# A two-layer encoder trunk on one core: down projections of two pairs each, the last pair's plain products added into the same banks, and two of four weight sums written by a plain and an accumulating transfer

## The chip, the core and the metric

The kernel runs on one core of a Trainium2 chip. Its engines each work through a queue of their own in program order: TensorE (PE; PEld is its loading of weights) does matmuls into PSUM, VectorE (DVE) and ScalarE (ACT) work element by element, GpSimd (POOL) does little here, and SyncE (SP) issues transfers. The metric is the device time of one execution in microseconds; less is better.

## The reference

Two groups of tokens (512 and 256) of width 1024 go through two layers with shared weights. Each layer is a half feed-forward block, a mixer (gated spatial mixing beside windowed attention in the first layer, neighbourhood attention in the second) and another half feed-forward block; a final norm ends it. The change concerns the four feed-forward blocks:

```python
def rmsnorm(x, g):
    x32 = x.astype(jnp.float32)
    y = x32 * lax.rsqrt(jnp.mean(x32 * x32, axis=-1, keepdims=True) + EPS)
    return y.astype(x.dtype) * g
...
def swiglu(h, wg, wu, wd):
    return (jax.nn.silu(h @ wg) * (h @ wu)) @ wd
...
    x = x + 0.5 * swiglu(rmsnorm(x, f1_n), f1_g, f1_u, f1_d)
```

`wg` and `wu` are 1024 x 2816, `wd` is 2816 x 1024, all in float32.

## The kernel before

**Numbers.** A float32 operand is split into a rounded part (hi) and the remainder (lo), and each product is three matmuls: hi x hi, hi x lo, lo x hi (`mm3`, L184). A weight is split by `wsplit` (L105): ScalarE copies to `whi`, VectorE subtracts to `wlo`. There are five buffers of each, so splits run a few products ahead.

**Layout.** x lies transposed, features on the partitions in 8 tiles `x0` to `x7` of 768 tokens. The tokens are two halves of 384 (`HALVES`); all matmuls of the blocks have 384 columns.

**Pairs.** The 2816 hidden features are 11 pairs of 128-wide tiles. For a pair, the gate and the up projection are each a 2 x 2 block product (two halves of the 1024 inputs by two tiles, two halves of tokens), done in 7 products in place of 8, with sums on both sides: operand sums `t1`, `t2`, `t3`, `n4` beside the plain `b11`, `b21`, `b22` (made once per block by `feed` and `rest`), and weight sums s1 = a21 + a22, s2 = s1 - a11, s3 = a11 - a21, s4 = a12 - s2 (`sums`, L577), where a11 to a22 are 512 columns (a quarter) of the weights. A product of one projection is 12 matmuls (4 x `mm3`); `p1` to `p7` do both projections. s1 and s2 are made when `p6` (operand t2) asks for s2, s3 for `p7`, s4 for `p3`; s1 is used in `p5`. The seven results are joined in the banks X, Y, Z and in SBUF tiles, and `hidden` (L474) makes silu(gate) x up for each quarter of the pair's hidden values; it reads the bank of the last product (`sg<-ps_mm`, `v<-ps_mm`).

**Order.** TensorE's order is as written; the other engines' order comes from a scheduler. The first three pairs (`EARLY`) do their plain products `p1`, `p2` first, for all three, while the sums on the operand side are still being made; then their other five products follow pair by pair. Generators (`rest`, `second`, `norm_rt`) are advanced between products.

**Down.** Hidden values are summed and split per pair by `operands` (L400). `down` (L599) does 7 products per pair with the same four weight sums, accumulating over its pairs in one bank: pair 0 alone after pair 1, then pairs (1,2), (3,4), (5,6), (7,8), each two pairs later. Z is kept in `acc` over all of them and added to x by `last_operands` (L650). Pairs 9 and 10 go through `down_last` (L664) with plain products: for each of 8 output tiles and 2 halves 4 x `mm3` in an aux bank, then `x` is updated and `final` (L695) does what the next stage needs (the norm's squares, and the next operands: `feed` before a feed-forward block, `xh`/`xl` before a mixer). `half_done` then spawns the norm's tail, in which POOL takes a power (L254) and TensorE transposes its result (`ident,sm`).

**Loads.** Each 128 x 1024 weight tile comes as one 512 KB transfer on SP into one of four `raw` buffers (`raw`, L88). The sums lie in 8 buffers `s`.

Of the kernel before, what the change touches and what calls it, by code (L numbers as in the profile page):

```python
# [15 lines left out]
P = 128  # L16
# [32 lines left out]
class Trunk:  # L49
# [55 lines left out]
    def wsplit(self, src, eng=None, keep=False):  # L105
# [8 lines left out]
        hi, lo = (t.rearrange("p (a b) -> p a b", a=src.shape[1]) for t in (hi, lo))  # L114
        nc.scalar.copy(hi, src)  # L115
# [181 lines left out]
    def feed(self, m, h):  # L297
# [17 lines left out]
        if k in self.tmp and k + 4 in self.tmp:  # L315
            t2 = self.tmp["t2", k] = self.etile("tmp")
            self.combine(t2, self.tmp[k], -1, k, self.tmp[k + 4])
# [4 lines left out]
    def gain_split(self, n, k, src, m):  # L322

        hi, lo = self.b[n][k]
        self.nc.scalar.activation(hi, src, AF.Copy, scale=self.gain(m))
        self.nc.vector.scalar_tensor_tensor(
            out=lo, in0=src, scalar=self.gain(m), in1=hi.bitcast(F32), op0=ALU.mult, op1=ALU.subtract
        )

    def combine(self, out, x, sign, m, other):  # L330

        g, op = (self.gain(m), ALU.subtract) if sign > 0 else (self.gain(m, self.ngains), ALU.add)
# [11 lines left out]
    def rest(self, after):  # L344
# [5 lines left out]
        for n in ("t3", "t1", "b22", "n4"):  # L350
            for k in range(4):
                with self.tc.issue_after(self.copied[after - 1]) if after else nullcontext():
# [6 lines left out]
                    elif n == "n4":  # L359
                        t = self.tmp["t2", k]  # L360
                        self.combine(t, self.x[k + 4][:, a0:a1], 1, k + 4, t)
# [27 lines left out]
    def ffn(self, pre):  # L389
# [8 lines left out]
        d, dl = {}, {}  # L398

        def operands(q):  # L400
# [3 lines left out]
            sub = lambda o, x, y: nc.vector.tensor_tensor(out=o, in0=x, in1=y, op=ALU.subtract)  # L404
            d[q] = {}

            def put(n, src):
                d[q][n] = self.dtile(n), self.dtile(n)
# [4 lines left out]
            yield sub(h11, h12, h11)  # L413
            yield put("t1", h11)
            yield put("b21", h21)
            yield sub(h11, h22, h11)
            if q and q % 2 == 0:
                self.later = operands_2(h, sub, put)
                return
            for _ in operands_2(h, sub, put):  # L420
                yield

        def operands_2(h, sub, put):
# [5 lines left out]
            yield sub(h21, h21, h11)  # L429
            yield put("n4", h21)  # L430

        def pair(p):
# [5 lines left out]
            def load(tiles):  # L438
                for n in names:
                    for i in tiles:  # L440
                        r = self.first.pop(0) if self.first else self.raw(f"{pre}_w_{n}", 0, KD, (2 * p + i) * P, P)
                        a[n, i + 1, 1], a[n, i + 1, 2] = r[:, 0:4, :], r[:, 4:8, :]
# [5 lines left out]
            def sums(n, name):  # L448
                return self.sums(a[n, 1, 1], a[n, 1, 2], a[n, 2, 1], a[n, 2, 2], s, n, name)
# [24 lines left out]
            def hidden(i, half, g, u):  # L474
# [6 lines left out]
                nc.scalar.activation(t, t, AF.Silu)  # L481
                nc.vector.tensor_tensor(out=v, in0=u, in1=r, op=ALU.mult)
                nc.vector.scalar_tensor_tensor(out=t, in0=t, scalar=0.5, in1=v, op0=ALU.mult, op1=ALU.mult)  # L483
# [60 lines left out]
            load((0, 1))  # L544
            if p:
                steps = operands(p - 1) if p < NPAIR - 1 else self.last_operands(dl, 0, hs[p - 1], acc)
# [10 lines left out]
        for p in range(NPAIR):  # L557
            for _ in stages[p]:
                pass
            if p == 1:  # L560
                acc += [self.fw.tile([P, H], F32, tag=f"p1{j}", name=f"p1{j}") for j in range(4)]
            if p % 2 and p < NPAIR - 1:
# [1035 lines left out]
```

## Time and profile before

| | |
|---|---|
| median of 3 runs | 2640.08 us (2638.77 to 2641.93) |
| the profiled execution | 2645.25 us, of it the span of the program 2643.5 us |
| granted TensorE clock, mean | 0.993 |
| TensorE busy | 2586.7 us (98%), 15180 matmuls |
| VectorE busy | 2225.4 us (84%) |
| ScalarE busy | 1357.5 us (51%) |
| POOL busy | 97.6 us (4%) |
| transfers | 214.27 MB, mean 81 GB/s |

A row of a group names the line, engine, operation, out<-in and shape, then the count, busy time, mean ns of one, and the idle time of the engine just before them with what ended it. `L141` is the line of every matmul, so matmuls are told apart by tiles: `t20h,whi` is the rounded weight against the rounded operand t2 of input tile 0, the first matmul of that product. In a row of the timeline stand start, duration, engine, line and, in brackets, the idle time before it.

### The profile page before, as it was taken

To read this page: it belongs to the slowest core of one execution; us is meant where nothing else is said; L and a number is where in the kernel's file an instruction comes from. 1 tells how busy PE (TensorE), PEld (TensorE's weight loads), DVE (VectorE), ACT (ScalarE), POOL (GpSimd) and SP (SyncE) were. 2 spreads that over 40 slices of the span, in tenths; PEclk is the share of its full clock that TensorE was granted. 3 is DMA by queue.
4 is the path that set the end of the run, shared out by engine and by line. 5 is a ranking of instruction groups with operands and counts; after the bars stand their busy time and mean duration, and the time that the engine had idled before them with its cause. 6 is when DMAs were issued, how large, how long until landed. Compare 5 with 4: busy or idle time off the path is not lost.

```text
span 2643.5 us, 40905 instructions
## 1 busy us (share of the span) xinstructions
PE 2586.7 (98%) x15180; PEld 2515.4 (95%) x15180; DVE 2225.4 (84%) x4447; ACT 1357.5 (51%) x2808; POOL 97.6 (4%) x139
## 2 busy tenths in 40 slices
PE   8999999999999999999999999999999999999998
PEld 7899999987898999999999999998998989999998
DVE  8988889878869988889898888985667589888886
ACT  6545444546746544545654544464555455454443
POOL 0000000000000000000000000002212100000000
PEclk9999999999999999999999999999999999999999
DMA  5433222321132222223232222232112222222221
GB/s 156 125 81 93 80 73 71 126 89 51 47 101 91 80 65 79 67 78 96 64 96 64 76 69 75 69 129 80 60 62 72 80 80 80 80 65 80 64 81 63
DMA packets 83176, 214.27 MB, mean 81 GB/s; under 512 B 20128, under 2 KB 32928, under 8 KB 82976
## 3 DMA queue, kind: packets, MB, share of 16 engines
q1 hardware_dynamic: 82832, 211.62, 25.8%
q8 instruction: 119, 1.95, 0.3%
q14 instruction: 81, 0.66, 0.1%
q10 hardware_dynamic: 144, 0.03, 0.0%
HBM read 202.18 MB, written 15.07 MB: 82 GB/s over the span
## 4 chain that ended last, share of the span: by engine, by line
PE 68%; DVE 4%; ACT 2%; issue 1%; DMA 1%; POOL 0%; DVEq 0%; ACTq 0%; SPq 0%; POOLq 0%
PE ps_mm L141 42%; PE ps_aux L141 25%; PE ps_aux L152 1%; DMA raw<-in_w 1%; DVE wlo L116 1%; DVE s L579 1%; DVE ol L205 0%; ACT whi L115 0%; DVE tmp L333 0%; DVE x L631 0%; ACT ug L1157 0%; ACT L1157 0%; ACT p L884 0%; ACT L884 0%; DVE sg L483 0%
## 5 line engine op out<-in xcount | busy, mean ns | idle before, releaser
L115 ACT CAST whi<-s 128x512 fp32r<-128x512 f32 x496 | 301.7, 620 | 392.8 <-DVE s L579 142.8
L115 ACT CAST whi<-raw 128x512 fp32r<-128x512 f32 x512 | 312.5, 619 | 284.9 <-PE ps_mm L141 134.1
L116 DVE TENSOR_TENSOR wlo<-s,whi 128x512 fp32r<-128x512 f32 x496 | 336.0, 686 | 77.3 <-ACT whi L115 75.2
L116 DVE TENSOR_TENSOR wlo<-raw,whi 128x512 fp32r<-128x512 f32 x494 | 335.8, 686 | 38.6 <-ACT whi L115 35.9
L141 PE MATMUL ps_mm<-db,whi 128*128 128x384 f32 x864 | 221.3, 337 | 0.0
L141 PE MATMUL ps_aux<-dt,whi 128*128 128x384 f32 x864 | 221.3, 337 | 0.0
L141 PEld LDWEIGHTS ps_aux<-dt,whi 128*128 128x128 f32 x864 | 156.8, 188 | 0.0
L141 PEld LDWEIGHTS ps_mm<-db,whi 128*128 128x128 f32 x864 | 156.8, 188 | 0.0
L141 PE MATMUL ps_aux<-dt,wlo 128*128 128x384 f32 x432 | 145.7, 337 | 0.4 <-DVE wlo L116 0.4
L141 PE MATMUL ps_mm<-db,wlo 128*128 128x384 f32 x432 | 145.6, 337 | 0.0
L141 PE MATMUL ps_mm<-xh,whi 128*128 128x512 f32 (+1 forms) x416 | 145.3, 349 | 0.0
L141 PE MATMUL ps_mm<-xl,whi 128*128 128x512 f32 (+1 forms) x416 | 141.0, 339 | 0.0
L141 PE MATMUL ps_mm<-xh,wlo 128*128 128x512 f32 (+1 forms) x416 | 140.9, 339 | 0.0
L466 ACT COPY u<-ps_mm 128x384 f32<-128x384 f32 x176 | 83.5, 475 | 41.6 <-PE ps_mm L141 41.4
L471 DVE TENSOR_TENSOR u<-ps_aux,u 128x384 f32<-128x384 f32 x176 | 97.3, 553 | 6.9 <-PE ps_aux L141 4.5
L579 DVE TENSOR_TENSOR s<-raw 128x512 f32<-128x512 f32 x124 | 85.1, 686 | 17.3 <-DMA raw<-in_w 17.2
L579 DVE TENSOR_TENSOR s<-raw,raw 128x512 f32<-128x512 f32 x124 | 83.3, 686 | 19.4 <-DMA raw<-in_w 19.4
L141 PE MATMUL ps_aux<-dh,whi 128*128 128x384 f32 x384 | 98.9, 339 | 0.0
L631 DVE TENSOR_TENSOR x<-ps_aux,x 128x384 f32<-128x384 f32 x160 | 86.9, 554 | 12.3 <-PE ps_aux L141 12.2
L884 ACT ACTIVATE p<-p,st 128x256 f32<-128x256 f32 (+3 forms) x144 | 69.1, 481 | 47.8 <-DVE st L879 47.7
L631 DVE TENSOR_TENSOR x<-ps_mm,x 128x384 f32<-128x384 f32 x160 | 87.1, 552 | 6.0 <-PE ps_mm L141 6.0
L141 PEld LDWEIGHTS ps_mm<-xh,whi 128*128 128x128 f32 x416 | 78.9, 190 | 9.8 <-issue 1.0
(477 smaller groups left out, 8030.8 us busy)
## 6 DMA issues: line engine op xcount, KB each, us to landing
raw<-in_w SPq DMA_DIRECT2D x338, 512.0 KB, 3.7
xdm<-x SPq DMA_DIRECT2D x16, 384.0 KB, 2.4
raw<-in_w SPq DMA_DIRECT2D x16, 256.0 KB, 4.0
x<-in_x SPq DMA_DIRECT2D x16, 192.0 KB, 4.6
xold<-xdm SPq DMA_DIRECT2D x8, 384.0 KB, 3.0
x<-xdm SPq DMA_DIRECT2D x8, 384.0 KB, 3.5
out_y<-y SPq DMA_DIRECT2D x8, 384.0 KB, 2.6
tab<-skew SPq DMA_DIRECT2D x8, 256.0 KB, 4.2
```

Source lines behind the costliest of these rows:

```text
L115: nc.scalar.copy(hi, src)
L116: (eng or nc.gpsimd).tensor_tensor(out=lo, in0=src, in1=hi.bitcast(F32), op=ALU.subtract)
L141: self.nc.tensor.matmul(out, lhsT=lhsT, rhs=rhs, start=start, stop=stop, **kw)
L152: self.nc.tensor.transpose(out, src, self.ident)
L466: nc.scalar.copy(e[n, out], bank[key, n])
L471: nc.vector.tensor_tensor(out=t, in0=bank[key, n], in1=t, op=ALU.add)
L579: f = lambda o, x, y, op: self.nc.vector.tensor_tensor(out=o, in0=x, in1=y, op=op)
L631: nc.vector.tensor_tensor(out=o, in0=ps, in1=o, op=ALU.add)
L884: nc.scalar.activation(outs[i - n0], outs[i - n0], AF.Exp, scale=-1.0, bias=mn[:, i : i + 1], accum_out=sm[:, i : i + 1])
```

## The change

**Sums by transfer.** s1 and s3 are no longer made on VectorE: SP loads one quarter into a buffer `s`, and POOL issues a second transfer that adds the other quarter to it in memory. Signs are changed so that every sum is an addition: s2 = s1 + a11 and s4 = a12 + s2 stay on VectorE, s3 = a11 + a21, and the operand sums t1, t2, n4, the hidden values of a pair's second tile and the outputs of tiles 4 to 7 carry the sign. A quarter that is used in a sum and by itself is loaded for each use; `region` names a weight region without loading it, and `parts` loads quarters into a `raw` buffer.

**Down in twos.** `down` runs after pairs 2, 4, 6 and 8 for pairs (0,1), (2,3), (4,5), (6,7). `down_last` does pairs (8,9) in 7 products and adds the plain products of pair 10 into the same banks before these are read. Z is kept for the earlier pairs only, and is added to half 1 of x by `steps_last`. `out` calls `final`, as `one` did. Before a feed-forward block or the last norm (`lag`) the order is as written below; before a mixer it is other.

```diff
+    def region(self, name, k0, nk, c0, n):
+        size = P * nk * n
+        self.units.append((name, k0, nk, c0, n))
+        src = self.aps["w"][self.woff : self.woff + size].rearrange("(p f) -> p f", p=P)
+        self.woff += size
...
+        return src
+    def parts(self, *srcs):
+        raw = self.rawp.tile([P, 512 * len(srcs)], F32, tag="raw", name=f"rawp{len(self.units)}")
+        for i, src in enumerate(srcs):
+            self.nc.sync.dma_start(raw[:, i * 512 : (i + 1) * 512], src)
...
+    def wsum(self, name, x, y):
+        t = self.fw.tile([P, 4, P], F32, tag="s", name=name, bufs=8)
+        f = t.rearrange("p a b -> p (a b)")
+        self.nc.sync.dma_start(f, x)
+        self.nc.gpsimd.dma_start(f, y, accum_op=ALU.add)
+        return t
...
+            def load_all():
...
+                for n in names:
+                    a[n, 1, 1], a[n, 1, 2] = self.parts(q[n, 1, 1], q[n, 1, 2])
+                for n in names:
+                    s[n, "s1"] = self.wsum("s1", q[n, 2, 1], q[n, 2, 2])
+                for n in names:
+                    s[n, "s3"] = self.wsum("s3", q[n, 1, 1], q[n, 2, 1])
+                a["gate", 2, 2], a["up", 2, 2] = self.parts(q["gate", 2, 2], q["up", 2, 2])
...
-            if p % 2 and p < NPAIR - 1:
-                self.down(pre, range(max(p - 2, 0), p), d, acc)
+            if p and p % 2 == 0 and p < NPAIR - 1:
+                self.down(pre, range(p - 2, p), d, acc)
...
-        self.down_last(pre, dl)
+        self.down_last(pre, range(NPAIR - 3, NPAIR - 1), d, hs[NPAIR - 1])
...
         if name == "s2":
-            t = s[n, "s1"] = self.fw.tile([P, 4, P], F32, tag="s", name="s1", bufs=8)
-            f(t, a21, a22, ALU.add)
+            t = s[n, "s2"] = self.fw.tile([P, 4, P], F32, tag="s", name=name, bufs=8)
+            f(t, s[n, "s1"], a11)
+        elif name == "s4":
+            f(s[n, "s2"], a12, s[n, "s2"])
...
+        def plain(st, half, key, j):
...
+            for i in (0, 1):
+                self.mm3(
+                    bank[key, j], (st[i][0][:, j, :], st[i][1][:, j, :]), dl[i, half], new and i == 0, i == 1, not new
+                )
...
+        def out(m, half, key):
+            add(m, half, bank[key, m % 4])
+            self.final(m, *HALVES[half])
...
+        def fifth():
+            st = split(sums("s1"))
+            for j in range(4):
+                part(st, "t1", "Z", j, True)
+                add(4 + j, 1, bank["Z", j])
+        def third(u):
+            st = {p: self.wsplit(s4[p], nc.vector, lag and p == pairs[1]) for p in pairs}
+            for j in range(4):
+                part(st, "b22", "Z", j, False)
+                plain(u, 1, "Z", j)
+                out(j, 1, "Z")
...
+            fifth()
+            third(lasts(0))
+            seventh()
```

**What moves, at three places.** The first is VectorE in the first block, at the step from pair 0 to pair 1. `sg<-ps_mm` and `v<-ps_mm` read the banks of pair 0's last product; `s1`, `s2`, `s3` are the weight sums of pair 1 (gate, then up), `wlo` the remainders of split weights. Before:

```order
L483 SCALAR_TENSOR_TENSOR u2_591<-u2_591,u2_619 128x384
L116 TENSOR_TENSOR wlo37_798<-raw9_563,whi37_797 128x512
L480 TENSOR_TENSOR sg_813<-ps_mm22_565,acc_165 128x384
L579 TENSOR_TENSOR s1_829<-raw11_821 128x512
L579 TENSOR_TENSOR s2_831<-s1_829,raw10_819 128x512
L482 TENSOR_TENSOR v_814<-ps_mm24_593,acc_165 128x384
L483 SCALAR_TENSOR_TENSOR sg_813<-sg_813,v_814 128x384
L116 TENSOR_TENSOR wlo39_834<-s2_831,whi39_833 128x512
L579 TENSOR_TENSOR s2_831<-raw10_819,s2_831 128x512
L579 TENSOR_TENSOR s1_857<-raw13_825 128x512
L579 TENSOR_TENSOR s2_859<-s1_857,raw12_823 128x512
```

Now, from the same split on:

```order
L147 TENSOR_TENSOR wlo37_803<-rawp10_575,whi37_802 128x512
L631 TENSOR_TENSOR s2_847<-s1_830,rawp14_824 128x512
L631 TENSOR_TENSOR s2_873<-s1_833,rawp14_827 128x512
L534 TENSOR_TENSOR sg_818<-ps_mm22_578,acc_165 128x384
L147 TENSOR_TENSOR wlo39_850<-s2_847,whi39_849 128x512
L147 TENSOR_TENSOR wlo41_876<-s2_873,whi41_875 128x512
L147 TENSOR_TENSOR wlo42_895<-s3_836,whi42_894 128x512
L536 TENSOR_TENSOR v_819<-ps_mm24_604,acc_165 128x384
L147 TENSOR_TENSOR wlo43_917<-s3_839,whi43_916 128x512
L537 SCALAR_TENSOR_TENSOR sg_818<-sg_818,v_819 128x384
L147 TENSOR_TENSOR wlo45_940<-s1_830,whi45_939 128x512
```

The two sums s2 of pair 1 now stand ahead of the first read of a bank, and no s1 and no s3 is among the rows.

The second is POOL in the first block: `sm` are the powers for the norms of the two halves, then of the mixer (`mv`: the layer norm's). Before, with nothing in between:

```order
L1443 TENSOR_SCALAR ngains_93<-gains_91 128x56
L254 TENSOR_TENSOR sm_329<-sm_329,minus_87 128x3
L254 TENSOR_TENSOR sm_686<-sm_686,minus_87 128x3
L254 TENSOR_TENSOR sm_5707<-sm_5707,minus_87 128x6
L254 TENSOR_TENSOR mv_6382<-mv_6382,minus_87 128x3
L254 TENSOR_TENSOR mv_6885<-mv_6885,minus_87 128x3
```

Now:

```order
L1599 TENSOR_SCALAR ngains_93<-gains_91 128x56
L285 TENSOR_TENSOR sm_329<-sm_329,minus_87 128x3
L127 DMA s1_563<-in_w 128x512
L127 DMA s1_566<-in_w 128x512
L127 DMA s3_569<-in_w 128x512
L127 DMA s3_572<-in_w 128x512
L127 DMA s1_830<-in_w 128x512
L127 DMA s1_833<-in_w 128x512
L127 DMA s3_836<-in_w 128x512
L127 DMA s3_839<-in_w 128x512
L285 TENSOR_TENSOR sm_691<-sm_691,minus_87 128x3
```

The accumulating transfers of pairs 0 and 1 (s1 and s3, for gate and up) stand between the two powers.

The third is VectorE in the last down of the second layer's first block, where the outputs of half 1 leave. `x0`, `x1`, `x2` are output tiles, `acc` the norm's sum of squares, `xl` the remainders for the mixer. Before, while tiles 4 to 6 leave:

```order
L676 TENSOR_TENSOR x5_7668<-ps_aux1356_18924,x5_7668 128x384
L676 TENSOR_TENSOR x4_7667<-ps_aux1357_18941,x4_7667 128x384
L228 TENSOR_TENSOR acc_18684<-acc_18684,sq_18938 128x384
L116 TENSOR_TENSOR wlo1366_19179<-raw244_19172,whi1366_19178 128x512
L228 TENSOR_TENSOR acc_18684<-acc_18684,sq_18955 128x384
L708 SCALAR_TENSOR_TENSOR xl4_18701<-x4_7667,gains_91,xh4_18693 128x448
L708 SCALAR_TENSOR_TENSOR xl4_18701<-x4_7667,gains_91,xh4_18693 128x64
L708 SCALAR_TENSOR_TENSOR xl4_18701<-x4_7667,gains_91,xh4_18693 128x256
L676 TENSOR_TENSOR x6_8092<-ps_aux1359_18970,x6_8092 128x384
```

Now, where tiles 0 to 2 leave ahead of the product with s3:

```order
L147 TENSOR_TENSOR wlo1319_19045<-s2_18801,whi1319_19044 128x512
L147 TENSOR_TENSOR wlo1320_19135<-s3_18793,whi1320_19134 128x512
L760 TENSOR_TENSOR x0_7624<-ps_mm1312_19000,x0_7624 128x384
L864 SCALAR_TENSOR_TENSOR xl0_18770<-x0_7624,gains_91,xh0_18762 128x448
L864 SCALAR_TENSOR_TENSOR xl0_18770<-x0_7624,gains_91,xh0_18762 128x64
L864 SCALAR_TENSOR_TENSOR xl0_18770<-x0_7624,gains_91,xh0_18762 128x256
L760 TENSOR_TENSOR x1_7625<-ps_mm1313_19008,x1_7625 128x384
L259 TENSOR_TENSOR acc_18757<-acc_18757,sq_19081 128x384
L760 TENSOR_TENSOR x2_7748<-ps_mm1314_19016,x2_7748 128x384
L864 SCALAR_TENSOR_TENSOR xl1_18771<-x1_7625,gains_91,xh1_18763 128x448
L864 SCALAR_TENSOR_TENSOR xl1_18771<-x1_7625,gains_91,xh1_18763 128x64
L864 SCALAR_TENSOR_TENSOR xl1_18771<-x1_7625,gains_91,xh1_18763 128x256
```

Both halves of a tile left in turn before; now only half 1 leaves here, its remainders are three rows a tile, and of the two splits of s3 the first (wlo1320) stands ahead of them, the second behind the remainders of tile 2.

More of the change, by code (lines that the diff above doesn't have):

```diff
@@ L633, in more @@
         def more(n):
[L634 removed]
+            for _ in range(n):
                 next(self.later, None)
[L637 removed]
         s2 = sums("s2")
```

252 lines of the change are left out of this document (169 added, 83 removed).

## The prediction

> **What bounds the kernel now.** I read the page first, then the chain of waits, then TensorE's instruction groups, and last the timeline at the places that those groups point to. The page's busy table (us, share of the span, instructions):
>
> ```profile
> PE 2586.7 (98%) x15180; PEld 2515.4 (95%) x15180; DVE 2225.4 (84%) x4447; ACT 1357.5 (51%) x2808; POOL 97.6 (4%) x139
> ```
>
> TensorE is busy 98% of the span, so time is saved in two ways only: fewer matmuls, or fewer places where a matmul waits. The price of a matmul comes from a long undisturbed piece of the chain of work that ended last:
>
> ```profile
> 981.28 21.20 PE ps_mm L141 x120
> ```
>
> That is 21.20 / 120 = 0.1767 us for one matmul of 384 columns. The groups of TensorE's matmuls (busy us, mean ns, then the idle time before them and who ended it) say where it waits most in the feed-forward blocks:
>
> ```profile
> L141 PE MATMUL ps_mm<-t20h,wlo 128*128 128x384 f32 x88 | 31.3, 356 | 5.4 <-DVE wlo L116 4.9
> L141 PE MATMUL ps_mm<-t20h,whi 128*128 128x384 f32 x88 | 30.9, 351 | 13.9 <-ACT whi L115 13.9
> ```
>
> This is before the first two matmuls of the product with t2, whose weight is the sum s2: 13.9 + 5.4 = 19.3 us, ended by ScalarE's rounded copy and VectorE's remainder of that sum. The timeline shows why, at the step from pair 0 to pair 1 of the first block (start, duration; TensorE, then VectorE, then ScalarE):
>
> ```profile
> 74.02 0.44 PE L141 MATMUL ps_mm<-t20h,whi 128*128 128x384 f32 x1 [0.33 <-ACT whi L115]
> ...
> 75.61 0.44 PE L141 MATMUL ps_mm<-t20h,wlo 128*128 128x384 f32 x1 [0.97 <-DVE wlo L116]
> ...
> 79.14 0.44 PE L141 MATMUL ps_mm<-t20h,whi 128*128 128x384 f32 x1 [1.50 <-ACT whi L115]
> ```
> ```profile
> 71.38 0.56 DVE L480 TENSOR_TENSOR sg<-ps_mm,acc 128x384 f32<-128x384 f32 x1 [2.34 <-PE ps_mm L141]
> 71.85 0.68 DVE L579 TENSOR_TENSOR s<-raw 128x512 f32<-128x512 f32 x1
> 72.57 0.69 DVE L579 TENSOR_TENSOR s<-s,raw 128x512 f32<-128x512 f32 x1
> 73.73 0.56 DVE L482 TENSOR_TENSOR v<-ps_mm,acc 128x384 f32<-128x384 f32 x1 [0.47 <-PE ps_mm L141]
> ...
> 74.87 0.68 DVE L116 TENSOR_TENSOR wlo<-s,whi 128x512 fp32r<-128x512 f32 x1
> ...
> 76.92 0.69 DVE L579 TENSOR_TENSOR s<-s,raw 128x512 f32<-128x512 f32 x1
> ```
> ```profile
> 73.35 0.62 ACT L115 CAST whi<-s 128x512 fp32r<-128x512 f32 x1 [0.85 <-DVE s L579]
> ```
>
> VectorE runs in program order. It stood 2.34 us behind the read of a bank that TensorE had not finished (71.38), and the two sums of the next pair (71.85, 72.57) were queued behind that read; the sum for "up" came only at 76.92. Three waits of 0.33, 0.97 and 1.50 us follow.
>
> **The change part by part.**
>
> *Fewer matmuls.* A block has 11 pairs. Before, 9 go through down in 7 products (84 matmuls each) and 2 plainly (96 each): 948. After, 10 and 1: 936. That is 12 less, four times: 48 x 0.1767 = 8.5 us, all on the bounding engine. Sure.
>
> *Two of four sums leave VectorE.* The transfers now write s1 and s3, VectorE makes s2 and s4. A sum costs:
>
> ```profile
> L579 DVE TENSOR_TENSOR s<-raw 128x512 f32<-128x512 f32 x124 | 85.1, 686 | 17.3 <-DMA raw<-in_w 17.2
> ```
>
> The change's sums number 256 where before's number 496, so 240 x 0.686 = 165 us leave an engine that is busy 84%. In a steady pair that is worth nothing, because nothing waits there: the first row below has no TensorE idle. Of its 30 us VectorE works 25.15; the second row is pair 1, where it works 23.99 of 25.
>
> ```profile
> 225.00:255.00 30.00, 30.00 (x172) 30.00 (x172) 25.15 (x46) 13.76 (x28) 0.00 (x0) 1.00 0.37 115
> 74.00:99.00 25.00, 22.33 (x122) 21.37 (x123) 23.99 (x45) 13.44 (x27) 0.00 (x0) 1.00 0.37 117
> ```
>
> It is worth something only in the first pairs of each block. There the order above shows both s2 sums of pair 1 now standing ahead of the blocking read, which is their place because s1 comes ready from memory. So the three waits there should go, and their like. How much of the 19.3 us is of this kind? The first pair of two blocks is another kind: there a sum stands in a full queue of operand splits, and only one of two sums ahead of each cast goes. Those windows:
>
> ```profile
> L141 PE MATMUL ps_mm<-t20h,wlo 128*128 128x384 f32 x2 | 1.0, 514 | 0.4 <-DVE wlo L116 0.4
> L141 PE MATMUL ps_mm<-t20h,whi 128*128 128x384 f32 x2 | 0.8, 389 | 3.0 <-ACT whi L115 3.0
> ```
> ```profile
> L141 PE MATMUL ps_mm<-t20h,wlo 128*128 128x384 f32 x2 | 0.9, 444 | 1.5 <-DVE wlo L116 1.4
> L141 PE MATMUL ps_mm<-t20h,whi 128*128 128x384 f32 x2 | 0.8, 390 | 0.5 <-ACT whi L115 0.5
> ```
>
> They hold 0.4 + 3.0 + 1.5 + 0.5 = 5.4 us, of which I take two sums of 0.686 in each block, 2.7 us. The other 13.9 us stand at steps from pair to pair; I take 12.3 of it, leaving about one wait of 1.5 us. Together 15 us; bounds 6 (only half of the steps gain) and 19.3.
>
> *The clock.* Behind such waits TensorE's granted clock falls. Two windows (the third last column is the clock) around steps between pairs:
>
> ```profile
> 830.00:845.00 15.00, 12.01 (x55) 10.73 (x55) 13.17 (x23) 5.87 (x12) 0.00 (x0) 0.89 0.30 103
> 2180.00:2190.00 10.00, 8.15 (x37) 7.51 (x36) 8.72 (x15) 5.39 (x11) 0.00 (x0) 0.83 0.36 107
> ```
>
> They lose 0.11 x 15 = 1.65 and 0.17 x 10 = 1.7 us. If the waits go, these 3.3 us go too; bounds 0 and 3.3.
>
> *The transfers.* Each quarter that goes into a sum is now loaded by 256 KB transfers, and POOL issues the second of each sum when the first has landed. The nearest rows for landing (us at the end), and for one POOL instruction:
>
> ```profile
> tab<-skew SPq DMA_DIRECT2D x8, 256.0 KB, 4.2
> ```
> ```profile
> L254 POOL TENSOR_TENSOR sm<-sm,minus 128x3 f32<-128x3 f32 (+1 forms) x12 | 13.7, 1144 | 1608.1 <-DVE sm L253 1608.1
> ```
>
> No row shows an accumulating transfer. I take 4.2 + 1.1 + 4.2 = 9.5 us from free buffer to sum, with 8.4 us for the second landing as the far end (13.7 us). [...] The cover: in the order of the changed kernel the tightest sum (s1 of pair 2) has 97 matmuls between the one that frees the queue ahead of it and the one that needs the sum, 97 x 0.1767 = 17.1 us; most have over 120 (21 us). A pair moves 14 quarters of 256 KB where it moved 8; the transfer engines, busy 0.37 of the steady window above, would be busy 0.37 x 14 / 8 = 0.65 of it: hidden. I cost this at nothing; if the cover fails, see the second rival.
>
> *POOL's queue.* In the first block the power for the norm of the second half now stands behind eight transfers, the last of which needs the buffer of s1 (the wlo below is its last reader). TensorE transposes its result at a fixed place:
>
> ```profile
> 53.73 0.68 DVE L116 TENSOR_TENSOR wlo<-s,whi 128x512 fp32r<-128x512 f32 x1
> ```
> ```profile
> 56.59 1.23 POOL L254 TENSOR_TENSOR sm<-sm,minus 128x3 f32<-128x3 f32 x1 [32.06 <-DVE sm L253]
> ```
> ```profile
> 59.43 0.49 PE L152 MATMUL ps_aux<-ident,sm 128*128 128x128 f32 x3
> ```
>
> 54.4 + 4.2 (landing) + 1.1 (issue) + 1.2 (power) = 60.9 against 59.4: 1.5 us of wait, bounds 0 and 4. In the other blocks the last transfer ahead stands further away.
>
> *The last down.* Ten x 84 + 96 matmuls keep the rate, but VectorE gets more outputs per matmul: t2, t3 and t1 are each added to x on their own. In the second layer's first block, while four outputs of half 1 leave (48 matmuls, 8.5 us; the last 42 of them, 7.4 us, behind the first output), VectorE has these to do per output:
>
> ```profile
> L676 DVE TENSOR_TENSOR x<-ps_aux,x 128x384 f32<-128x384 f32 x16 | 8.9, 554 | 2.9 <-PE ps_aux L141 2.9
> ...
> L708 DVE SCALAR_TENSOR_TENSOR xl<-x,gains,xh 128x448 fp32r<-128x448 f32 x8 | 5.5, 683 | 0.5 <-ACT xh L707 0.5
> L708 DVE SCALAR_TENSOR_TENSOR xl<-x,gains,xh 128x256 fp32r<-128x256 f32 x8 | 3.8, 479 | 0.0
> L708 DVE SCALAR_TENSOR_TENSOR xl<-x,gains,xh 128x64 fp32r<-128x64 f32 x8 | 2.2, 280 | 0.0
> ```
>
> Add and norm 2 x 0.554, remainders 1.44: 2.55 us against 12 matmuls of 2.12 us, so 1.7 us short over four, and the splits of s3 (2 x 0.69) are queued among them: about 3 us there before TensorE gets s3. In the three other blocks I take nothing, since what TensorE wants next from VectorE lies further off. So 3 us; bounds 0 and 9.
>
> **Sum.** -8.5 - 15 - 3.3 + 1.5 + 3 = -22.3 us. The profiled execution took 2645.25 us (span 2643.5), 5.2 us over the median 2640.08 of the runs, so 2623 there and 2618 for the median.
>
> **The rivals.**
>
> 1. *VectorE is blocked by POOL's issuing* (slower). The change puts 256 issues on an engine that stood idle in these blocks. If an issue holds VectorE for as long as a POOL instruction (1.144 us), each costs more than the sum that it replaces (0.686); that is the point from which it decides. A first pair then has 4 x (1.144 - 0.686) = 1.8 us more VectorE work than now where it has 1 us spare (23.99 of 25), and the waits grow instead of going: 12 first pairs x 1.8 = 22 us, less 8.5, so +13.5 plus the 4.5 of POOL's queue and the last down: 2640 + 18 = 2658. For it: in the two mixers, where POOL does its sums, one VectorE group reaches four times its median (shortest, median, longest in ns):
>
> ```profile
> L893 DVE TENSOR_SCALAR p<-p,st x144: 291/346/1390, 571.5 to 2059.0; 128x256 f32<-128x256 f32 x64, 128x192 f32<-128x192 f32 x32, 128x160 f32<-128x160 f32 x32, 128x384 f32<-128x384 f32 x16
> ```
>
> Against it: those are sums on POOL with operands of their own, not issues, and the median is undisturbed. [...]
> 2. *The wait moves to the landing.* If the accumulating landing takes over 17.1 - 4.2 - 1.1 = 11.8 us, the cover of pair 2, which is as short in three blocks, is used up, and VectorE, which now has the s2 sum early in its queue, stands behind the transfer with everything else. At 4 us a block: 2618 + 12 = 2630. Against it: a plain landing of that size takes 4.2 us.
> 3. *The last down is bound by VectorE in all four blocks.* From the code it has 18 splits (0.69), 24 adds and 16 norm adds (0.554), 8 outputs' remainders (1.44) and some 11 smaller steps (0.6): 52.7 us against 264 matmuls, 46.6 us. If nothing slides into its neighbours, 6 us x 4 in place of 3: 2618 + 21 = 2639. Against it: the stage after starts on half 0 and has its own cover.
> 4. *The change removes less than it says.* The order excludes it: TensorE has 48 matmul rows less.
>
> **How the numbers follow.** Forecast 0.72, rival 1 0.09, rival 2 0.12, rival 3 0.07. The forecast's own bounds: -8.5 - 19.3 - 3.3 = -31 gives 2609; -8.5 - 6 + 4 + 9 = -1.5 gives 2639, its far end. The range 2608 to 2637 takes in nearly all of the forecast, rival 2 and a milder rival 3. A difference of 0.2%, 5.3 us, is about what a measurement of this kernel can tell from none. Faster than 2634.8: the forecast without its far end (0.70), rival 2, and a milder rival 3 (0.02), 0.84; slower than 2645.4: rival 1, 0.09; between, the rest of rival 3 and of the forecast, 0.07.
>
> **What would show it.** The sum group of VectorE should fall to 256, the t20h groups' idle time from 19.3 to about 4 us, the clock should stay 1.00 around the second block's pair steps, and TensorE's rows of 384 columns should lessen by 48. A wait of TensorE before ident,sm near 60 us, longer than 4, or before the product with t3 in the last downs, would make the middle terms wrong. VectorE rows of 512 columns well over 686 ns beside POOL's issues would be rival 1; VectorE idle behind an accumulating transfer would be rival 2. A time over 2637 is a failure of the forecast whatever its cause.

## The result, and the profile after

The changed kernel takes 2618.77 us in the median (2613.74 to 2622.39, 4 runs) against 2639.6 us (2638.77 to 2641.93): ratio 0.9917, 95% interval 0.9905 to 0.9929. Measured once more later it took 2619.4 against 2641.32 us, ratio 0.9909 (0.9892 to 0.9926). So it is faster by 20.8 to 21.9 us; the forecast was 2618. The profiled execution took 2613.74 us (span 2611.9), 5.0 us under its median, where that of the kernel before lay 5.2 us over its own: the two traces differ by 31.5 us, of which some 10 belong to the two executions and not to the kernels. Sizes below are therefore read from idle times and checked against medians.

The page's busy table of the changed kernel (us, share, instructions), and TensorE's groups where it waits in the blocks (busy us, mean ns, idle before and who ended it):

```profile
PE 2566.2 (98%) x15132; PEld 2500.5 (96%) x15132; DVE 2103.4 (81%) x4211; ACT 1373.9 (53%) x2828; POOL 321.6 (12%) x395
```
```profile
L172 PE MATMUL ps_mm<-n40h,wlo 128*128 128x384 f32 x88 | 30.2, 343 | 4.8 <-DVE wlo L147 4.8
L172 PE MATMUL ps_mm<-t20h,wlo 128*128 128x384 f32 x88 | 30.2, 343 | 1.6 <-DVE wlo L147 1.6
...
L172 PE MATMUL ps_aux<-b220h,whi 128*128 128x384 f32 x88 | 30.0, 341 | 3.5 <-DVE u L525 2.7 <-ACT whi L146 0.8
L172 PE MATMUL ps_mm<-t20h,whi 128*128 128x384 f32 x88 | 30.0, 341 | 2.2 <-ACT whi L146 2.1
...
L172 PE MATMUL ps_mm<-t30h,whi 128*128 128x384 f32 x88 | 29.7, 338 | 0.0
...
L172 PE MATMUL ps_aux<-b210h,whi 128*128 128x384 f32 x8 | 3.1, 387 | 3.4 <-ACT p L550 3.4
```

The same groups of the kernel before, those that the prediction did not show:

```profile
L141 PE MATMUL ps_mm<-t30h,whi 128*128 128x384 f32 x88 | 30.4, 346 | 1.1 <-ACT whi L115 1.1
L141 PE MATMUL ps_mm<-n40h,wlo 128*128 128x384 f32 x88 | 30.0, 341 | 4.8 <-DVE wlo L116 4.8
L141 PE MATMUL ps_aux<-b220h,wlo 128*128 128x384 f32 x88 | 30.0, 341 | 2.6 <-DVE wlo L116 2.6
...
L141 PE MATMUL ps_aux<-b210h,whi 128*128 128x384 f32 x8 | 2.9, 365 | 1.8 <-ACT p L496 1.8
```

48 matmuls are gone, and the wait for s2 (t20h) fell from 19.3 to 1.6 + 2.2 = 3.8 us. Three things are to be seen beside it. n40h kept its 4.8 us. Before the product with b22 TensorE now waits 3.5 us, 2.7 of it for `u` of VectorE, where it waited 2.6 for a remainder. And b210h grew from 1.8 to 3.4 us. VectorE's sums are down to 256 (the 128 of s2 below and as many of s4), and POOL's issues stand in their place (the three transfer rows of the page end in KB each and us to landing):

```profile
L631 DVE TENSOR_TENSOR s<-s,rawp 128x512 f32<-128x512 f32 x128 | 87.6, 688 | 13.1 <-DMA rawp<-in_w 8.3
...
L127 POOL DMA_DIRECT2D s<-in_w x256 | 223.5, 905 | 1476.4 <-DVE sg L433 323.6
...
rawp<-in_w SPq DMA_DIRECT2D x384, 256.0 KB, 3.9
s<-in_w SPq DMA_DIRECT2D x256, 256.0 KB, 3.1
s<-in_w POOLq DMA_DIRECT2D x256, 256.0 KB, 5.0
```

The step from pair 0 to pair 1 of the first block, VectorE: both s2 sums now stand ahead of the read `sg` of TensorE's bank, which waits 0.15 us where it waited 2.34:

```profile
67.44 1.29 DVE L631 TENSOR_TENSOR s<-s,rawp 128x512 f32<-128x512 f32 x2
68.88 0.56 DVE L534 TENSOR_TENSOR sg<-ps_mm,acc 128x384 f32<-128x384 f32 x1 [0.15 <-PE ps_mm L172]
```

Busy time by windows (us; TensorE, its loads, VectorE, ScalarE, POOL; then the granted clock, the share of the transfer engines and GB/s): the steady pair, the two steps whose clock the prediction quoted, and a third place:

```profile
225.00:255.00 30.00, 30.00 (x173) 30.00 (x172) 23.72 (x43) 14.10 (x28) 4.34 (x5) 1.00 0.72 165
817.00:832.00 15.00, 14.07 (x78) 13.10 (x77) 12.29 (x23) 9.55 (x21) 3.50 (x4) 1.00 0.88 216
2148.00:2158.00 10.00, 9.86 (x56) 9.86 (x57) 9.97 (x19) 6.32 (x13) 1.75 (x2) 1.00 0.63 196
```
```profile
2120.00:2128.00 8.00, 6.61 (x29) 6.62 (x30) 7.98 (x17) 7.83 (x16) 0.00 (x0) 0.79 0.82 223
```

In this execution the clock is 1.00 at both steps, as forecast, but 0.79 behind the longer b210h wait at 2121. The kernel moves 315.04 MB where it moved 214.27; the transfer engines are busy 0.72 of the steady window (0.65 was worked out from 14 / 8 quarters), with TensorE never idle in it.

Who makes the new waits shows in the timeline of the last block, VectorE and TensorE:

```profile
2110.73 0.69 DVE L631 TENSOR_TENSOR s<-s,rawp 128x512 f32<-128x512 f32 x1 [6.03 <-DMA rawp<-in_w]
...
2148.94 0.68 DVE L147 TENSOR_TENSOR wlo<-rawp,whi 128x512 fp32r<-128x512 f32 x1
...
2161.97 0.69 DVE L631 TENSOR_TENSOR s<-s,rawp 128x512 f32<-128x512 f32 x1 [2.73 <-DMA s<-in_w]
```
```profile
2121.39 0.44 PE L172 MATMUL ps_aux<-b210h,whi 128*128 128x384 f32 x1 [3.10 <-ACT p L550]
```
```profile
2166.41 0.44 PE L172 MATMUL ps_aux<-b220h,whi 128*128 128x384 f32 x1 [1.50 <-DVE u L525]
```

Twice VectorE stands at an s2 sum before its transfers have landed, for 6.03 us at pair 0 and 2.73 us at pair 2, and what is queued behind the sum reaches ScalarE and TensorE late. At pair 2 the row names the sum's own buffer: this is the second rival of the prediction, on a small scale. At pair 0 it names `rawp`, the plain quarter a11 that is loaded beside the sums, and so do 8.3 of the 13.1 us that VectorE idles before its s2 sums in all; no rival of the prediction had that.

### The profile page after: what moved, and what is told of

Read it like the earlier page. It is cut to its first block, busy times and chain, and to the rows that moved or that the text cites. A ratio compares the mean times of both kernels' runs of the same rounds, so it can differ in the third digit from the quotient of the medians.

```text
span 2611.9 us, 41975 instructions
## 1 busy us (share of the span) xinstructions
PE 2566.2 (98%) x15132; PEld 2500.5 (96%) x15132; DVE 2103.4 (81%) x4211; ACT 1373.9 (53%) x2828; POOL 321.6 (12%) x395
## 2 busy tenths in 40 slices
DMA packets 175345, 315.04 MB, mean 121 GB/s; under 512 B 30368, under 2 KB 43168, under 8 KB 175136
## 4 chain that ended last, share of the span: by engine, by line
PE 69%; DVE 3%; ACT 1%; issue 1%; DMA 1%; POOL 0%; DVEq 0%; ACTq 0%; POOLq 0%
PE ps_mm L172 45%; PE ps_aux L172 23%; PE ps_aux L183 1%; DVE wlo L147 1%; DMA raw<-in_w 0%; DVE ol L236 0%; DVE tmp L366 0%; DMA s<-in_w 0%; DMA rawp<-in_w 0%; DVE s L631 0%; ACT ug L1313 0%; ACT whi L146 0%; ACT L1313 0%; ACT p L1040 0%; ACT L1040 0%
## 5 line engine op out<-in xcount | busy, mean ns | idle before, releaser
L127 POOL DMA_DIRECT2D s<-in_w x256 | 223.5, 905 | 1476.4 <-DVE sg L433 323.6
L146 ACT CAST whi<-rawp 128x512 fp32r<-128x512 f32 x336 | 206.1, 619 | 253.1 <-PE ps_mm L172 103.4
L147 DVE TENSOR_TENSOR wlo<-rawp,whi 128x512 fp32r<-128x512 f32 x336 | 230.8, 687 | 25.0 <-ACT whi L146 17.7
L172 PE MATMUL ps_mm<-db,whi 128*128 128x384 f32 x944 | 242.2, 337 | 0.0
L172 PEld LDWEIGHTS ps_mm<-db,whi 128*128 128x128 f32 x944 | 171.2, 188 | 0.0
L146 ACT CAST whi<-raw 128x512 fp32r<-128x512 f32 x172 | 105.1, 619 | 93.3 <-PE ps_mm L172 71.2
L147 DVE TENSOR_TENSOR wlo<-raw,whi 128x512 fp32r<-128x512 f32 x154 | 104.4, 687 | 25.1 <-ACT whi L146 23.7
L631 DVE TENSOR_TENSOR s<-s,rawp 128x512 f32<-128x512 f32 x128 | 87.6, 688 | 13.1 <-DMA rawp<-in_w 8.3
L172 PEld LDWEIGHTS ps_mm<-db,wlo 128*128 128x128 f32 x472 | 88.6, 188 | 1.5 <-DVE wlo L147 1.5
L535 ACT ACTIVATE u<-u 128x384 f32<-128x384 f32 x88 | 46.3, 526 | 79.4 <-DVE u L534 79.4
```

The source lines that it names most:

```text
L127: self.nc.gpsimd.dma_start(f, y, accum_op=ALU.add)
L147: (eng or nc.gpsimd).tensor_tensor(out=lo, in0=src, in1=hi.bitcast(F32), op=ALU.subtract)
L172: self.nc.tensor.matmul(out, lhsT=lhsT, rhs=rhs, start=start, stop=stop, **kw)
L535: nc.scalar.activation(t, t, AF.Silu, scale=-1.0 if i else 1.0)
L631: f = lambda o, x, y: self.nc.vector.tensor_tensor(out=o, in0=x, in1=y, op=ALU.add)
```

## The experiments

Three theories were on the table. A, the place: the sums cost time only in the first three pairs, where they stand between a blocked read of VectorE and a cast that TensorE waits for. B, the load: VectorE's 165 us of sums count wherever they are. C: the matmuls and the new last down brought the gain, and the sums nothing. All ten runs, with the mean granted clock over a kernel's timed executions and the idle time of three groups (whi and wlo together, n40h wlo alone) in the profiled one:

| kernel | median us (runs) | ratio to before, 95% | clock | t20h | n40h | b220h |
|---|---|---|---|---|---|---|
| before (39 runs beside the others) | 2640.1 | | 0.9939 | 19.3 | 4.8 | 2.6 |
| changed, again (e5) | 2619.4 (4) | 0.9909 (0.9892 to 0.9926) | 0.9933 | 3.8 | 4.8 | 2.6 |
| e1, pairs 0 to 2 on VectorE | 2638.36 (10) | 0.9992 (0.9982 to 1.0001) | 0.9927 | 19.4 | 4.8 | 2.6 |
| e2, the rest on VectorE | 2617.89 (4) | 0.9918 (0.9903 to 0.9932) | 0.9938 | 3.9 | 4.8 | 2.9 |
| e3, all on VectorE | 2637.61 (10) | 0.9994 (0.9984 to 1.0003) | 0.9931 | 18.2 | 4.8 | 2.6 |
| e4, all on POOL | 2724.89 (4) | 1.0327 (1.0312 to 1.0342) | 0.9868 | 39.7 | 7.4 | 8.4 |
| e6, s1 written first | 2618.75 (4) | 0.9912 (0.9897 to 0.9926) | 0.9935 | 4.3 | 4.8 | 3.8 |
| e7, seven buffers | 2635.58 (10) | 0.9980 (0.9970 to 0.9990) | 0.9929 | 4.3 | 4.8 | 11.3 |
| e8, e6 and late products | 2605.5 (4) | 0.9861 (0.9846 to 0.9876) | 0.9953 | 3.3 | 0.0 | 0.2 |
| e9, late products alone | 2606.16 (4) | 0.9879 (0.9862 to 0.9895) | 0.9948 | 4.1 | 0.0 | 0.7 |
| e10, second transfer not added (the sums are left out) | 2610.93 (4) | 0.9892 (0.9877 to 0.9907) | 0.9948 | 3.8 | 4.8 | 1.5 |

### Where the sums cost: e1, e2, e3

For the pairs in a set, the quarters come in plainly as before and VectorE makes s1 when s2 is asked for and s3 for `p7`; e2 and e3 do so in `down` too. The last down keeps its transfers. In these kernels' rows L638 is a sum s1 or s3 and L634 a sum s2 or s4.

```diff
             def load_all():
+                if p in (0, 1, 2):      # e2: 3 to 10 and down; e3: 0 to 10 and down
+                    load((0, 1))
+                    return
...
+        for m, x, y in (("s1", a21, a22),) if name == "s2" else (("s3", a11, a21),) if name == "s3" else ():
+            if (n, m) not in s:
+                t = s[n, m] = self.fw.tile([P, 4, P], F32, tag="s", name=m, bufs=8)
+                self.nc.vector.tensor_tensor(out=t, in0=x, in1=y, op=ALU.add)
```

> The changed kernel with s1 and s3 of pairs 0, 1 and 2 of each block made by VectorE from plainly loaded quarters (48 sums back); all other transfers as changed. Theory A, the place (sums cost only where they stand between a blocked read of VectorE and a cast that TensorE waits for, which is in these pairs): the idle time of the two t20h groups goes from 3.8 back to about 19 us, the half-speed stretches at the second block's steps come back, the time rises by 15 to 18 us to about 2634 (2630 to 2637). Theory B, the load (what counts is VectorE's busy time, wherever it is): 48 of 240 sums are a fifth, so about +2.5 us, 2621. Theory C (the 48 matmuls and the new last down brought it, the sums nothing): 2619.

> The opposite: s1 and s3 of pairs 3 to 10 and of the four downs in twos made by VectorE again (192 sums, 132 us of VectorE work back); pairs 0, 1 and 2 and the last down as changed. Theory A: nothing waits there, t20h stays near 4 us, 2619 (2616 to 2623). Theory B: four fifths of the sums' gain are lost, about +10 us, 2629 or more. Theory C: 2619.

> Both: all sums of the pairs and of the downs in twos on VectorE (240 back), so that of the change the two-pair downs and the gathered last pair stay. Theory A: as the first of these, 2634 (2630 to 2637), so 3 to 9 us under the kernel before, the 48 matmuls less what the last down costs. Theory B: 2631 or more. Theory C: 2619 to 2621.

TensorE's t20h groups of e1, then of e2:

```profile
L172 PE MATMUL ps_mm<-t20h,wlo 128*128 128x384 f32 x88 | 31.5, 358 | 6.2 <-DVE wlo L147 6.0
L172 PE MATMUL ps_mm<-t20h,whi 128*128 128x384 f32 x88 | 30.7, 349 | 13.2 <-ACT whi L146 13.1
```
```profile
L172 PE MATMUL ps_mm<-t20h,wlo 128*128 128x384 f32 x88 | 30.1, 342 | 1.7 <-DVE wlo L147 1.7
L172 PE MATMUL ps_mm<-t20h,whi 128*128 128x384 f32 x88 | 30.0, 341 | 2.2 <-ACT whi L146 2.2
```

VectorE at the step from pair 0 to pair 1 of e1, to be held against the rows of the changed kernel above:

```profile
71.34 0.56 DVE L537 TENSOR_TENSOR sg<-ps_mm,acc 128x384 f32<-128x384 f32 x1 [2.08 <-PE ps_mm L172]
71.82 0.68 DVE L638 TENSOR_TENSOR s<-raw 128x512 f32<-128x512 f32 x1
72.53 0.69 DVE L634 TENSOR_TENSOR s<-s,raw 128x512 f32<-128x512 f32 x1
```

Theory A holds, B and C fall. 48 sums put back in pairs 0 to 2 cost 2638.36 - 2619.4 = 19 us, all of the sums' gain; 192 sums put back elsewhere, four times as much work for VectorE, cost nothing (2617.89). In e1 the sums are again queued behind a read that waits 2.08 us. Against e2, measured beside it, e1 costs 20.5 us. Its 2638.36 lies just above the 2630 to 2637 expected. What the runs show is that the place costs; whether the sums could have stayed on VectorE, ahead of the read that waits, was not tried. e3 gives what the downs in twos are worth alone: 2.4 us under the kernel before, an interval of -4.2 to +0.8 us from its ratio; 3 to 9 had been expected.

### Who should make them: e4

```diff
-                self.nc.vector.tensor_tensor(out=t, in0=x, in1=y, op=ALU.add)
+                self.nc.gpsimd.tensor_tensor(out=t, in0=x, in1=y, op=ALU.add)
```

> The same loads as the third, but the 240 sums are made by POOL instead of VectorE. If what matters is only that the sums leave VectorE's order (theory A): s1 comes one POOL instruction (about 1.3 us, from the POOL remainder row of 1296 ns) after the landing, VectorE's rows of 512 columns stay at 687 ns, and the time is 2619 to 2627. If POOL's reading of memory holds VectorE up (the mechanism of the first rival, which the issues did not show): VectorE's rows of 512 columns beside such a sum go to 1 us and more, the mean of the group rises well over 687, and the time is 2635 or more.

Groups of e4 on POOL and VectorE, and VectorE's remainders (shortest, median, longest in ns):

```profile
L638 POOL TENSOR_TENSOR s<-raw,raw 128x512 f32<-128x512 f32 x120 | 185.5, 1560 | 363.7 <-DMA raw<-in_w 333.0 <-DVE u L537 25.2 <-DVE u L528 5.5
```
```profile
L634 DVE TENSOR_TENSOR s<-s,raw 128x512 f32<-128x512 f32 x120 | 118.4, 987 | 152.8 <-POOL s L638 152.8
```
```profile
L147 DVE TENSOR_TENSOR wlo<-s,whi x510: 671/685/1853, 46.1 to 2689.1; 128x512 fp32r<-128x512 f32 x170
```

The same row of the changed kernel, with 256 issues on POOL:

```profile
L147 DVE TENSOR_TENSOR wlo<-s,whi x510: 676/686/695, 42.7 to 2579.9; 128x512 fp32r<-128x512 f32 x170
```

What the first rival feared is there, but beside POOL's sums and not beside its issues. Of e4's 1000 remainders on VectorE the 80 that overlap a sum of POOL take 1207 ns in the mean and up to 1853, and none of the others takes over 699; the s2 sum takes 987 ns in the mean. In the changed kernel none of the 197 remainders that overlap an issue of POOL takes over 695. VectorE also waits 152.8 us for POOL's sums, and the kernel is 105 us slower than with transfers; how much of that is the longer rows and how much the waits was not separated. Whether POOL's reading of memory is what lengthens them, as the expectation put it, these rows do not tell.

### What the transfers cost: e6, e7, e10

e6 writes the transfers of s1 ahead of those of a11 and a12:

```diff
             for n in names:
-                a[n, 1, 1], a[n, 1, 2] = self.parts(q[n, 1, 1], q[n, 1, 2])
-            for n in names:
                 s[n, "s1"] = self.wsum("s1", q[n, 2, 1], q[n, 2, 2])
+            for n in names:
+                a[n, 1, 1], a[n, 1, 2] = self.parts(q[n, 1, 1], q[n, 1, 2])
```

e7 has one buffer `s` less, and e10 writes the second transfer over the first, so that it leaves the sums out:

```diff
-        t = self.fw.tile([P, 4, P], F32, tag="s", name=name, bufs=8)
+        t = self.fw.tile([P, 4, P], F32, tag="s", name=name, bufs=7)
```
```diff
-        self.nc.gpsimd.dma_start(f, y, accum_op=ALU.add)
+        self.nc.gpsimd.dma_start(f, y)
```

> The changed kernel once more, on the chip of the next three, as their base. Both theories: 2615 to 2622.

> The changed kernel with one thing moved: for each pair the transfers of s1 are queued ahead of the plain quarters a11 and a12 instead of behind them. In the changed kernel VectorE stands 2.30 us (block 2, at 830) and 2.73 us (block 4, at 2162) before the s2 sum of pair 2, behind a transfer, and TensorE then waits 1.4 and 1.7 us before the product with b22. If the s1 chain is late because its first transfer stands behind the plain quarters (the second rival of the prediction, small): s1 lands 1 to 2 us earlier, both VectorE idles fall under 1 us, both TensorE waits go, 3 us less than the changed kernel. If it is late because its buffer comes free late, or because the accumulating landing itself takes 7 us there: no change.

> The changed kernel with 7 buffers for the sums instead of 8. By the order, the matmuls between the one that frees the queue ahead of an s1 sum of pair 2 and the one that needs it fall from 97 to 73 in blocks 2 and 4 (17.1 to 12.9 us), and some thirty sums of steady pairs now have 97 (17.1 us). If the chain of two landings takes about 11.4 us (2150.55 to 2161.97 in the changed kernel): steady pairs stay hidden, pair 2 of two blocks loses up to 4 us each, 5 to 8 us more than the changed kernel. If the cover of 17.1 us is already used up in steady pairs: 30 us more. If transfers are hidden anyhow: no change.

> The changed kernel with the second transfer of each sum written plainly over the first instead of added to it (s1 then holds a22 and s3 holds a21: the sums are left out). POOL issues the same 256 transfers, in the same order and with the same waits. In the changed kernel an accumulating transfer lands 5.0 us after its issue, a plain one by SP 3.1 us. If adding costs the difference (the memory is read as well as written): POOL's transfers land in about 3.5 us, VectorE's waits at pair 2 of blocks 2 and 4 shrink by 1.5 us each, 3 us less in all, 2616. If the path through POOL's queue costs it: 5.0 us again and 2619.

SP's queue ahead of pair 2 of the last block in e6, then two of TensorE's groups in e7:

```profile
2142.62 9.79 SPq L119 DMA_DIRECT2D rawp<-in_w  x4
2152.47 0.90 SPq L126 DMA_DIRECT2D s<-in_w  x2
```
```profile
L172 PE MATMUL ps_aux<-b220h,whi 128*128 128x384 f32 x88 | 31.2, 355 | 11.1 <-DVE u L525 10.1 <-ACT whi L146 0.8
...
L172 PE MATMUL ps_mm<-dh,klo 128*128 128x384 f32 x32 | 11.0, 343 | 3.3 <-DVE klo L147 3.3
```

POOL's issues and the landings in e10, and its b210h group:

```profile
L127 POOL DMA_DIRECT2D s<-in_w x256 | 138.4, 540 | 1549.8 <-DVE sg L433 339.2 <-DVE wlo L147 290.8 <-DVE u L433 185.3
```
```profile
s<-in_w POOLq DMA_DIRECT2D x256, 256.0 KB, 3.3
```
```profile
L172 PE MATMUL ps_aux<-b210h,whi 128*128 128x384 f32 x8 | 3.0, 377 | 1.1 <-ACT p L550 1.1
```

e6 is a miss: no time, and VectorE still waits 3.26 us (at 2164). But it does not answer its question. The order of SP's queue comes from the scheduler, and in the program's order the edit changed it in the first block only; ahead of pair 2 of the last block the plain quarters still go first, as in the changed kernel (2140.90 and 2150.55 below). What it would gain to have s1 first in the queue stays open. e7 costs 16.2 us (2635.58 - 2619.4) where 5 to 8 were expected: b220h stands at 11.3 us, 8.7 more than in the repeat, through `u` behind a late s2 sum, and the last downs, whose kept weights (`klo`) share these buffers, wait 3.3 us; the other 4 are not accounted for. Every wait of b220h over 0.3 us stands in the first pairs of a block (at 62, 109, 842, 2186 and 2210), none in a steady pair: 17.1 us of cover is enough there. e10 answers what the adding costs: with it alone taken away, POOL's issue falls from 905 to 540 ns and the landing from 5.0 to 3.3 us, where a plain one by SP had 3.1. So adding, not POOL's queue, makes nearly all of the difference (1.7 of 1.9 us), and it was not free; whether through the reading of the memory, as the expectation has it, no run shows. b210h falls to 1.1 us (3.4 in the first profile, 4.2 in the repeat) and b220h to 1.5 (3.7 and 2.6). The median is 8.5 us under the repeat's; the two were measured at different times, and by their gains over the kernel before beside each (28.6 and 21.9 us) it is 6.7. The two groups explain 4.2 to 4.5 of that; the clock, 0.0015 higher, up to 3 (at 2.1 us per 0.001, worked out below).

### What is still to be had: e8, e9

In the changed kernel the products that make the hidden values of half 1 of pair 0 stand in VectorE's queue ahead of the remainders of a22, although `down` needs them only after pair 2. e9 puts them behind the first products of pair 1; e8 is e9 and e6.

```diff
+            def late(*args):
+                if p == 0:
+                    behind.append(lambda: hidden(*args))
+                else:
+                    hidden(*args)
...
-                hidden(1, 1, e["gate", "u3"], e["up", "u3"])
+                late(1, 1, e["gate", "u3"], e["up", "u3"])
...
-                hidden(0, 1, e["gate", "u2"], e["up", "u2"])
+                late(0, 1, e["gate", "u2"], e["up", "u2"])
...
-        def operands(q):
+        behind = []
+        def operands(q, first=()):
+            if first:
+                yield
+                yield
+            while first:
+                yield first.pop(0)()
```

> The sixth with one more move: in pair 0 of each block the eight products of VectorE and ScalarE that make the two hidden tiles of the second half (needed only by the down after pair 2) are put behind the first sums of pair 1. In the changed kernel they stand ahead of the remainders of a22, and TensorE waits 4.8 us in the n40h,wlo group for those. If only their place makes that wait: n40h,wlo falls under 2 us, and with the sixth's gain the time is about 6 to 8 us under the changed kernel, 2611. If VectorE is simply full over pairs 0 and 1: what goes at n40h comes back at t20h of pair 1, and the time is that of the sixth.

> The eighth without the sixth's move: only the products of the second half of pair 0 are put behind the first sums of pair 1. The sixth alone moved nothing, so if the two moves do not lean on each other this gives the eighth's time, 2605 to 2607, with n40h,wlo at 0 us; if the early s1 chain is needed for it, something between 2606 and 2619, with VectorE idle behind a transfer in pair 1.

2605.5 us, 13.9 under the changed kernel of the same session: more than the 6 to 8 expected, and e9 shows that the late products do it alone. Both waits go at once, as the table shows, n40h from 4.8 to 0.0 and b220h from 2.6 (3.7 in the first profile) to 0.2, and t20h gives nothing back, so VectorE was not full over pairs 0 and 1; it did things in the wrong order. Why b220h goes too is seen in the next section. The granted clock, 0.9953, goes with most of the rest (0.0020 x 2.1 = 4 us). It is the fastest version here. The largest wait left in the blocks is b210h, 4.4 us in e8 and 4.0 in e9, which the late products don't touch; e10, where it is 1.1, points to the adding transfers for most of it.

## Why the prediction was right, point by point

**Fewer matmuls, -8.5, and the last down, +3.** 15180 matmuls became 15132. The last down waits where that was forecast, in the second layer's first block before the product with t3, and hardly elsewhere (0.27 us in the first block). It costs 2.0 us there, where 3 were taken:

```profile
1728.48 0.44 PE L172 MATMUL ps_mm<-db,wlo 128*128 128x384 f32 x1 [0.37 <-DVE wlo L147]
...
1737.53 0.62 PE L172 MATMUL ps_aux<-dt,whi 128*128 128x384 f32 x2 [0.69 <-ACT whi L146]
...
1739.12 0.44 PE L172 MATMUL ps_aux<-dt,wlo 128*128 128x384 f32 x1 [0.96 <-DVE wlo L147]
```

0.37 + 0.69 + 0.96 = 2.0 us. Together -5.5 was forecast, and e3 measured -2.4. Its clock was 0.0010 lower than that of the runs beside it (0.9931 against 0.9941), which is 2.1 us; the rest lies within its interval. Part of that clock stands at the last down: behind these three waits the profiles of e3 and of the repeat have 0.79 over 8 us, a loss of 1.7 us, and the first profile has 1.00.

**The sums, -15.** The step that carried the forecast, and right in place and size: t20h lost 15.5 us, e1 and e3 give it back, e2 does not. At the steps from pair to pair 0.6 us is left, where 1.5 was to be left; in the two first pairs that the prediction showed, 3.2 of 5.4, where 2.7 was to be left.

**The clock, -3.3.** This step failed. "If the waits go, these 3.3 us go too" holds for the two windows quoted in the first profile (1.00 now), not for the kernel: its eight runs had 0.9933 in the mean, the kernel before 0.9939 (0.9936 beside the repeat), where 3.3 us would have been 0.0012 more. A stretch at half the clock that one execution shows (0.50 from 840 to 843 and from 2185 to 2188 in the profile of the kernel before) does not come with the wait before it every time. e1 has the waits of the second block's step back, 0.61, 1.50 and 0.90 us where the kernel before had 0.61, 1.50 and 0.78, but not the 0.89 behind them that its expectation wanted back (in the last block it has 0.83 again):

```profile
825.00:840.00 15.00, 11.88 (x64) 10.61 (x64) 13.72 (x25) 7.83 (x16) 0.00 (x0) 1.00 0.34 105
```

And n40h of the last block waits 1.89 us in the first profile and 1.90 in the repeat, e5; the clock in the 8 us around it (from 2147 and from 2156) is 1.00 in the one and 0.79 in the other. The repeat also has a stretch behind a wait of 4.00 us at the start of the second block, where a plain weight transfer landed late (ScalarE stood 4.90 us for it):

```profile
777.89 0.69 PE L172 MATMUL ps_mm<-b110h,whi 128*128 128x384 f32 x1 [4.00 <-ACT whi L146]
```
```profile
776.00:784.00 8.00, 6.11 (x20) 5.88 (x21) 5.34 (x10) 4.85 (x10) 0.00 (x0) 0.57 0.73 198
```

In the first profile the same place (772 to 780) waited 0.86 us and kept 1.00. What decides whether a wait has such a stretch behind it is not shown, and which waits cost one in the timed runs can't be told from these profiles.

**The transfers, 0.** This step failed too, and the second rival was right in kind, though not by its condition: it asked for a landing of over 11.8 us, and this one took at most 6.9 (2155.08 to 2161.97). The cover of 97 matmuls (17.1 us) was set against the chain of transfers alone, as if VectorE acted at once at both of its ends. In the last block it runs from the product that VectorE awaits at 2145.93 to b220h at 2166.41, and VectorE's rows stand at each end:

```profile
2145.93 0.56 DVE L525 TENSOR_TENSOR u<-ps_aux,u 128x384 f32<-128x384 f32 x1 [0.19 <-PE ps_aux L172]
...
2165.80 0.55 DVE L525 TENSOR_TENSOR u<-ps_aux,u 128x384 f32<-128x384 f32 x1
```

The remainder of a22 that frees the buffer ahead in SP's queue ran at 2148.94. SP could go on only then (of the four transfers in the first row below two start at 2140.90 and two at 2149.70), and POOL issued its first adding transfer of pair 2 at 2155:

```profile
2140.90 9.61 SPq L119 DMA_DIRECT2D rawp<-in_w  x4
2150.55 1.10 SPq L126 DMA_DIRECT2D s<-in_w  x2
```
```profile
2155.08 1.75 POOL L127 DMA_DIRECT2D s<-in_w  x2 [16.41 <-DVE wlo L147]
```

From 2150.55 to the sum at 2161.97 the chain took 11.4 us, between the 9.5 taken and the 13.7 of the far end. To that come 4.6 us before it (2145.93 to 2150.55), most of them VectorE's, and 4.4 us behind it (2161.97 to 2166.35), in which VectorE has the sum and six other instructions to do before the `u` that TensorE awaits: 20.4 us in all, for a cover of 17.1 and the 1.9 that TensorE itself stood at n40h, which leaves it 1.4 short; b220h waited 1.50. The remainder at 2148.94 stands next to the one that TensorE awaits at n40h (both are of a22), so the late products of e9, which bring the two forward to 2138.76 and 2139.83, end both waits. By e10 the adding costs 6.7 to 8.5 us in all, where 0 was forecast.

**POOL's queue, +1.5.** Not there. The last adding transfer ahead of the power was issued at 51.44, not at 58.6, since its buffer was one that s3 leaves (its remainder ran at 47.13) and not that of s1. The power then waited for VectorE (2.88 us) and not for POOL's queue, and TensorE's transpose did not wait (POOL, then TensorE):

```profile
51.44 0.88 POOL L127 DMA_DIRECT2D s<-in_w  x1 [0.34 <-DVE wlo L147]
55.20 1.19 POOL L285 TENSOR_TENSOR sm<-sm,minus 128x3 f32<-128x3 f32 x1 [2.88 <-DVE sm L284]
```
```profile
58.03 0.49 PE L183 MATMUL ps_aux<-ident,sm 128*128 128x128 f32 x3
```

**The sum.** From rows of the first profile: -8.5 (matmuls) - 15.5 (t20h) - 1.1 (t30h) + 1.1 (b220h) + 1.6 (b210h) + 2.0 (last down) = -20.4 us, against 20.8 and 21.9 measured. The repeat's rows give -20.7 by the same terms, and its late transfer at the start of the second block takes 3.4 of that back. That the forecast's -22.3 is so near is in part luck. Its two failed steps erred the same way: 3.3 us of clock did not come, and 2.7 us of new waits did, 6.0 us together. Smaller things made up for 4.1: no wait for POOL (1.5), t30h (1.1, in no term), a cheaper last down (1.0) and a little more at t20h (0.5). The range, 29 us wide, would have held the result with larger errors too.

**The other rivals.** The first is out by the 695 ns; with the sums themselves on POOL, VectorE's remainders beside them took 1207 ns in the mean (e4). The third is out: of four last downs, one waits.

## What to carry to other kernels

Work taken from an engine that is 84% busy is worth what it gives at the places where the bounding engine waits: here 48 sums were worth 19 us and 192 others nothing, so look for the wait first and count instructions after. A cover for a transfer is to be counted from the time at which the engine that frees its buffer really gets there, behind the work in its own queue, and up to the place where the user stands in its queue: here 9 of some 19 us went to that. And when an in-order engine is late at a step, look for work in front of it that nobody needs yet: moving eight instructions a block gained two thirds of what the whole change did. On the kernel before, which has the same n40h wait, that was not tried.

## What the runs showed of the hardware

A transfer of 256 KB that adds to its target took 905 ns to issue on POOL and 5.0 us to land in the changed kernel; the same one without adding, 540 ns and 3.3 us (e10); a plain one by SP into the same buffers, 3.1 us in the changed kernel.

A sum of 128 x 512 took POOL 1560 ns (e4) and VectorE 686 (the kernel before), and VectorE's remainders beside POOL's sums took 1207 ns in the mean and up to 1853 (e4).

One kernel's time went with its granted clock: of the ten runs of e1 the one at 0.995 took 2632.6 us, the two at 0.991 took 2641.75 and 2640.18. That is 8.4 us for 0.004, or 2.1 us per 0.001, and a line through the 39 runs of the kernel before gives 2.2. A longer wait stood beside a lower clock: the 8 us around the 4.00 us wait of the repeat had 0.57. These 8.4 us are as much as some of the effects told of here, and the reason why medians of several runs and not two traces are compared.
